# Clearing the pads on VectorE, and weight sums whose plain copies go through SyncE's queue

## The chip, the cores and the metric

The kernel runs on one core of a Trainium2 chip. The metric is the device time of one launch in microseconds. Before the change three runs took 1014.99, 1016.2 and 1018.35 us, so the median is 1016.2 us.

## What is computed

One layer of a streaming encoder over 512 frames and 16 learned meta positions, with a width of 1024. In the reference, cut to what matters here:

```
u = rmsnorm(h);  proj = u @ w_in                  # conv branch, q, k, v, z, decay, beta, gates
c = c_val * sigmoid(c_gate);  c = dwconv31(c);  y_conf = silu(layernorm(c)) @ w_conf_out
q, k, v = split(silu(dwconv4([q, k, v])));  q, k = l2norm(q), l2norm(k)       # 8 heads of 128
o = chunk_gated_delta_rule(q, k, v, g, beta)      # needs inverses of triangular matrices
y_dn = (rmsnorm(o) * silu(z)) @ w_dn_out
h = h + (sigmoid(gA) * y_conf + sigmoid(gB) * y_dn) @ w_out
u2 = rmsnorm(h);  f_gate, f_val = split(dwconv3(u2 @ w_up))
h = h + (silu(f_gate) * f_val) @ w_down;  out = rmsnorm(h)[16:]
```

Everything is fp32.

## The kernel before

**Products.** A weight tile of 128 by 1024 numbers (512 KB) is fetched by SyncE into one of three buffers `wr`. ScalarE rounds it into `wh`, VectorE subtracts to get the rest `wl` (two buffers of each), and TensorE forms a product from three parts: `wh` with the rounded activation, `wh` with its rest, and `wl` with the rounded activation. One weight is 48 matmuls over half of the positions each. In the trace `cv`, `cg`, `q`, `k`, `v`, `z`, `ga`, `y`, `up`, `dn` are accumulators of such products, `wP`, `kS`, `S`, `vp` and `o` belong to the delta rule.

**Sums of weights.** Most tile pairs of the FFN's up projection are formed from seven products in place of eight, and that needs sums of quarters of the weights. `presums` makes 19 such groups of sums in DRAM (tile `ws`) by DMAs alone: two plain copies of 512 KB from the input, then one accumulating copy of 512 KB and two of 256 KB, each behind the one before it. All are started by GpSimd. The sums are read back as weights only in the FFN.

**Pads.** The causal convolution over four positions (`conv4` for q, k and v; `out_raw` for the first seven) reads a row of 528 positions with four zeros ahead of it. The row is the tile `ra`; `G.memset(a[:, :PAD], 0.0)` clears the four on GpSimd, 23 times. VectorE's three multiply-adds `cv<-ra,par,cv` read the row.

**Inverses.** `inverses` solves the triangular matrices by blocks of 32 on VectorE; `grow(h0)` puts the blocks of four heads together (`mn<-DU` copies on GpSimd, then TensorE). After it the heads run: the chain through the state `S`, with `r` on VectorE between two matmuls.

**Order.** The code only records its operations. A planner (`Plan.order`) gives each operation a price and a priority and writes one fixed list per engine; `Plan.emit` issues all of them at L469, so every row of the trace carries that line. `BIAS` moves named parts of the work in priority, `LNP`, `IVP`, `UP` and `WP` are the offsets of the layer norm, the inverses, the normalised input and the weights' splitting, and `SWITCH` is what a change of ScalarE's table costs in the planner. `plan.after` holds an operation back in the planner alone: on the chip an instruction waits for its data, its buffer and what stands ahead of it on its engine or queue. The lines are L538 to L556 (`presums`), L733 (`out_raw`), L854 (`conv4`), L990 (`grow`) and L1210 (the call of `presums`, held by the last mask that GpSimd makes).

Of the kernel before, what the change touches and what calls it, by code (L numbers as in the profile page):

```python
# [30 lines left out]
FT = DFF // P  # L31
EPS = 1e-6
PAD = 4
# [116 lines left out]
AHEAD = {'PE': 3000, 'DVE': 3000, 'ACT': 3000, 'POOL': 400, 'SP': 400}  # L150
KEEP = {"p1": 1, "st": 1, "bt": 2}
STAY = 3000
SWITCH = 375

BIAS = {'tp': 3910, 'h0': 970, 'h2': 370, 'h4': 870, 'h6': 1960, 'sw': 30, 'k3': 0, 'iv': 2100, 'd0': 30, 'v4': 30, 'v2': 0, 'd7': -250, 'z1': 0, 't11': -410, 'z5': 600, 't7': 30, 'k0': 1000, 'ln': 250, 's7': -60, 'z0': -350, 'o2': 250, 'o5': -60, 'd5': -3630, 'g3': -30, 'd6': 0, 'd1': 130, 'k2': 1500, 'q7': -100, 'k5': 600, 's4': -2070, 'd4': -270, 'w3': -1630, 't2': -720, 'c5': -230, 't8': -500, 'v3': -1220, 'o4': -30, 'q6': -250, 'g4': -220, 't4': -600, 'o1': 50, 'q4': -660, 't9': -430, 'z2': -250, 'o0': 3630, 'g0': 0, 'q3': 100, 'q5': 0, 'c1': 30, 'c6': -130, 's1': -1370, 't15': 250, 't1': -540, 's3': 0, 'y0': 150, 't12': -500, 'o6': 850, 'o3': -600, 'k4': 30, 'w2': 2300, 't5': 30, 'v0': 0, 'y2': 0, 'g7': 900, 'g1': 1520, 's6': -940, 'z4': -1680, 't0': 600, 'w0': -430, 'tq': 1880, 't13': 0, 'z6': 30, 'y3': -440, 'd3': -250, 'q2': -130, 't6': 30, 'u18': 150, 't3': -60, 'u6': -230, 'u15': 0, 'u8': -250, 'u17': 100, 'c2': -160, 'g2': 880, 'u1': 0, 'u3': 0, 'u11': 30, 'k1': 0, 'v7': -570, 'w4': -1430, 'u4': -100, 'm4': 0, 'q1': -1780, 't14': -150, 'u9': 0, 'u10': -280, 'u13': 600, 'y7': -130, 'u5': -130, 'm1': 70, 'u20': 0, 'm5': 60, 'u16': 130, 'u12': -250, 'q0': -1500, 'c3': -400, 'u19': 0, 'u14': -250, 'u2': -30, 'v6': 30, 'y6': 30, 'm6': -100, 'z3': 0, 'm0': 0, 'y1': -70, 'y4': -30, 's0': 0, 'g6': 750, 'c4': 0, 'c0': 250, 's5': -1250, 't10': 0, 'm2': 0, 'y5': 0, 'm7': 350, 'm3': 40, 'o7': 0, 'v5': 100, 'k6': 0, 'v1': -250, 'u21': -100, 'd2': -1000, 'u7': 600, 'c7': 0, 'z7': 0, 'g5': 0, 'k7': -70}
LNP = -146
IVP = 2165
UP = 519
WP = 214


WARM = 16
# [21 lines left out]
NPRE = 3  # L184
# [46 lines left out]
class Plan:  # L231
# [10 lines left out]
    def at(self, by, late=True):  # L242
        if isinstance(by, str):
            by, late = BIAS.get(by, 0), False
        was = self.late
# [52 lines left out]
    def price(self, eng, fn, a, k, out):  # L298
        n = out.n
        if eng == "PE":  # L300
            lhs, rhs = (k["lhsT"], k["rhs"]) if fn == "matmul" else (a[1], a[2])
            n = rhs.n
            if fn == "transpose":
                return 110, 0
            if lhs.tl.dt == F32R:

                return RATE * n + 4 + (2 if rhs.ap.offset % rhs.tl.row % 4 else 0), 0
            return max(n, lhs.n) / 0.6 + 8, 0
        if fn == "dma_start":
            if eng == "POOL":  # L310

                return 1000, int(np.prod(out.shape)) * 4 / 140.0
            return 475, int(np.prod(out.shape)) * 4 / 290.0 * (1 if self.run(k) >= P else 2)
        aps = sum(isinstance(k.get(x), Vw) for x in ("scalar", "scalar1", "scalar2", "scale", "bias", "mul"))
        src = [v for x, v in k.items() if x.startswith("in") and isinstance(v, Vw)]
        psum = any(v.tl.space == "psum" for v in src + [out])
        if eng == "ACT":
            return 0.833 * n + (51 if any(v.tl.space == "psum" for v in src) else 93) + 93 * aps + 93 * ("accum_out" in k) + (124 if out.shape[0] in (32, 64) else 0), 0
        if eng == "DVE":
            r = {"reciprocal": 6.3, "tensor_copy": 1.04 if psum else 0.52, "tensor_scalar": 1.04 if psum else 0.52}.get(fn, 1.042)  # L320
            return r * n + 65 + 62 * aps + (134 if fn == "transpose" else 0), 0
        return 1.0 * n + 80, 0

    def order(self):
# [32 lines left out]
        def look(e, t):  # L357

            q, nxt, best = ready[e], later[e][0][0] if later[e] else None, None
            for p, i in q:  # L360
# [111 lines left out]
def record(A, out):  # L472
    plan = Plan(SLOTS)
    V, S, G, PE, SY = (Rec(plan, e) for e in ("DVE", "ACT", "POOL", "PE", "SP"))

    def ext(ap):
        t = Tl(plan, "dram", None, list(ap.shape), F32, "ext")
        t.real = ap
        return Vw(t, ap)

    A = {n: ext(ap) for n, ap in A.items()}
    out = ext(out)
# [4 lines left out]
    def bt(dt=F32, n="bt"):  # L487
        return plan.tile("sb", "bt", [P, ROW], dt, n)
# [21 lines left out]
    def pc(name, i=0, w=1):  # L510
        return par[:, COL[name] + i:COL[name] + i + w]


    def weights(src, n=D):
# [4 lines left out]
        lo = plan.tile("sb", "wl", [P, D], F32R, "wl")  # L519
        with plan.at(WP):  # L520
            S.copy(out=hi[:, :n], in_=w[:, :n])
# [16 lines left out]
    def presums(src, n, hold):  # L538


        r = [plan.tile("dram", "con", [P, 4, HD], F32, "ws") for _ in range(n)]
        for m in range(n):
          with plan.at(1):

            h = {hold} | ({softs[-2]} if len(softs) > 1 else set())
            plan.after = set(h)
            G.dma_start(out=r[m][:, 0:2], in_=src[:, m, 0:3:2])
            plan.after = set(h)
            G.dma_start(out=r[m][:, 2:4], in_=src[:, m, 0:2])
            G.dma_start(out=r[m][:, 1:3], in_=src[:, m, 3:4].broadcast_to([P, 2, HD]), accum_op=ALU.add)  # L550
            G.dma_start(out=r[m][:, 0], in_=r[m][:, 1], accum_op=ALU.add)
            G.dma_start(out=r[m][:, 3], in_=r[m][:, 0], accum_op=ALU.add)
            softs.append(len(plan.ops) - 1)
        return r
# [68 lines left out]
    def split(src, width, n="x"):  # L623
        hi, lo = bt(F32R, n + "h"), bt(F32R, n + "l")
        S.copy(out=hi[:, :width], in_=src)
        V.tensor_tensor(out=lo[:, :width], in0=src, in1=hi.bitcast(F32)[:, :width], op=ALU.subtract)
        return hi, lo
# [24 lines left out]
    def rstd_rows(ss, width, scale, bias, whole=False):  # L652

        q = width // 4
        acc, r = sums(ss, width, whole)
        S.activation(out=r[:, :q], in_=acc[:, :q], func=AF.Sqrt, bias=bias, scale=scale)
        V.reciprocal(out=r[:, :q], in_=r[:, :q])
        return r
# [4 lines left out]
    def halves(ap, w):  # L663
        return ap.rearrange("p (b w) -> p b w", b=2)
# [65 lines left out]

    def out_raw(acc):
        a = bt(n="ra")
        G.memset(a[:, :PAD], 0.0)  # L733
        V.tensor_tensor(out=halves(a[:, PAD:], 264), in0=acc[:, :, :264], in1=halves(rx[:, :T], 264), op=ALU.mult)
        return a

# [2 lines left out]
    for k in range(KT + 1):  # L739
      with plan.at(UP):  # L740
        if k < KT:
# [58 lines left out]
    g2 = g_.rearrange("p n h -> p (n h)")  # L800
# [46 lines left out]
    def conv4(acc, t, way=None):  # L847

        c = bt(n="cv")
        if way:  # L850
            a = acc
            if way == "copy":
                a = bt(n="ra")
                G.memset(a[:, :PAD], 0.0)  # L854
                S.copy(out=halves(a[:, PAD:], 264), in_=acc[:, :, :264])
            cv, src = c[:, :T], lambda j: a[:, 1 + j:1 + j + T]
        else:
            cv, src = halves(c[:, :T], 264), lambda j: acc[:, :, 1 + j:265 + j]
        S.mul(out=cv, in_=src(3), mul=pc('dw', t * 4 + 3))
        for j in (2, 1, 0):  # L860
            V.scalar_tensor_tensor(out=cv, in0=src(j), scalar=pc('dw', t * 4 + j), in1=cv, op0=ALU.mult, op1=ALU.add)
        S.activation(out=c[:, :T], in_=c[:, :T], func=AF.Silu)
        return c
# [76 lines left out]
        for b in range(4):  # L940
            SY.dma_start(out=d_m[b, h].rearrange("n j t -> j n t"), in_=mn[32 * b:32 * b + 32, :, 32 * b:32 * b + 32])

    masks, softs = [], []
    ivt = {}

    def inverses():
# [247 lines left out]
    def call(fn, name, i):  # L1194
        with plan.at(f"{name}{i}"):
            return fn(i)
# [9 lines left out]
    for h in (H - 2, H - 1):  # L1206
        call(decays, "d", h)
        call(grams, "m", h)

    wus = presums(A['wuq'], FT - NPRE, masks[-1])  # L1210
    with plan.at(IVP), plan.at("iv"):
        inverses()
    for f in range(max(sum(GLUS, [])) + 2, KT):
# [10 lines left out]
    for h in range(H):  # L1224
        heads(h)
        if h == 0:
            call(grow, "w", NG)
        for i in OUTS[h]:
            outs(i)
        for i in GATES[h]:  # L1230
            gts[i] = call(gate, "t", i)
# [29 lines left out]

    with plan.at(LNP), plan.at("ln"):
        layer_norm()
# [119 lines left out]
    for f in range(KT - 1):  # L1383
# [3 lines left out]
        o = back(f)  # L1387
# [9 lines left out]
    o, s = back(f), bt(n="fsq")  # L1397
    for b in range(2):
# [9 lines left out]
        r = rstd_rows([sq[:, c], s[:, c]], hw, 1.0 / D, eps)  # L1408
# [97 lines left out]
```

## Time and profile before

| | us |
|---|---|
| median of three runs | 1016.2 |
| the profiled execution | 1018.73 |
| its span | 1016.9 |
| TensorE busy in it | 995.6 |
| VectorE busy | 766.4 |
| ScalarE busy | 526.2 |
| GpSimd busy | 108.4 |

The mean granted clock of TensorE in that execution was 0.994 of full speed. TensorE is busy for 98% of the span, but a busy matmul may be one at a lower clock, or one whose recorded end is modelled; GpSimd's share counts its DMA starts, while the time in which it stands before a DMA for its data to land counts as idle. A part of a microsecond is to be had only where TensorE stands or is slow, so the rows further down are mostly those of such places.

### The profile page before, as it was taken

To read this page: it belongs to the slowest core of one execution; us is meant where nothing else is said; L and a number is where in the kernel's file an instruction comes from. 1 tells how busy PE (TensorE), PEld (TensorE's weight loads), DVE (VectorE), ACT (ScalarE), POOL (GpSimd) and SP (SyncE) were. 2 spreads that over 40 slices of the span, in tenths; PEclk is the share of its full clock that TensorE was granted. 3 is DMA by queue.
4 is the path that set the end of the run, shared out by engine and by line. 5 is a ranking of instruction groups with operands and counts; after the bars stand their busy time and mean duration, and the time that the engine had idled before them with its cause. 6 is when DMAs were issued, how large, how long until landed. Compare 5 with 4: busy or idle time off the path is not lost.

```text
span 1016.9 us, 20105 instructions
## 1 busy us (share of the span) xinstructions
PE 995.6 (98%) x8202; PEld 949.7 (93%) x8202; DVE 766.4 (75%) x1304; ACT 526.2 (52%) x945; POOL 108.4 (11%) x172
## 2 busy tenths in 40 slices
PE   9999999999999999999999999999999999999996
PEld 6999999999989998989999999999999999988886
DVE  5988959689979998989485455599998988832334
ACT  5688732263644554355373224467786766632222
POOL 0011221523421222120000000000000000000000
PEclk9999999999999999999999999999999999999998
DMA  6144698988688897883313244424555556643332
GB/s 224 63 124 97 174 208 218 254 161 191 178 152 203 217 221 158 206 195 87 123 63 110 98 167 138 133 84 145 176 179 184 189 164 185 206 136 101 99 93 83
DMA packets 67932, 157.39 MB, mean 155 GB/s; under 512 B 15104, under 2 KB 21632, under 8 KB 67840
## 3 DMA queue, kind: packets, MB, share of 16 engines
q1 hardware_dynamic: 51728, 116.26, 36.1%
q0 software_dynamic: 16112, 39.85, 20.4%
q8 instruction: 64, 1.05, 0.4%
q14 instruction: 28, 0.23, 0.1%
HBM read 150.78 MB, written 45.16 MB: 193 GB/s over the span
## 4 chain that ended last, share of the span: by engine, by line
PE 72%; DMA 12%; issue 6%; DVE 5%; ACT 3%; POOL 1%; SPq 0%; DVEq 0%; ACTq 0%; POOLq 0%
PE dn L469 12%; PE sx L469 10%; PE y L469 9%; DMA ws<-in_wuq 7%; PE sz L469 7%; PE wo L469 5%; PE cv L469 5%; PE ga L469 4%; PE cg L469 4%; PE up L469 3%; PE z L469 2%; PE v L469 2%; DMA ws<-ws 2%; DMA eg<-d_e 2%; PE q L469 2%
## 5 line engine op out<-in xcount | busy, mean ns | idle before, releaser
L469 DVE TENSOR_TENSOR wl<-wr,wh 128x1024 fp32r<-128x1024 f32 (+2 forms) x195 | 225.6, 1158 | 156.0 <-PE dn L469 61.6
L469 ACT CAST wh<-wr 128x1024 fp32r<-128x1024 f32 (+2 forms) x195 | 193.8, 996 | 222.0 <-PE dn L469 56.4
L469 DVE SCALAR_TENSOR_TENSOR ca<-c,par,ca 128x516 f32<-128x516 f32 (+10 forms) x240 | 178.4, 750 | 6.3 <-ACT ca L469 2.3
L469 DVE SCALAR_TENSOR_TENSOR uy<-up,par,uy 128x512 f32<-128x512 f32 x88 | 64.2, 746 | 1.8 <-ACT uy L469 1.4
L469 POOL DMA_DIRECT2D ws<-in_wuq x57 | 49.3, 872 | 151.3 <-DMA ws<-in_wuq 77.7
L469 PE MATMUL dn<-fh,wh 128*128 128x512 f32 (+1 forms) x171 | 61.8, 369 | 0.0
L469 PE MATMUL dn<-fl,wh 128*128 128x512 f32 (+1 forms) x171 | 61.8, 369 | 0.0
L469 PE MATMUL sx<-nh,wh 128*128 128x258 f32 x228 | 60.5, 289 | 1.2 <-ACT wh L469 0.9
L469 PE MATMUL sz<-nl,wh 128*128 128x258 f32 x228 | 59.8, 283 | 0.0
L469 PE MATMUL sx<-nl,wh 128*128 128x258 f32 x228 | 59.4, 282 | 0.0
L469 PE MATMUL sz<-nh,wh 128*128 128x258 f32 x228 | 59.4, 283 | 0.0
L469 PE MATMUL ga<-ul,wh 128*128 128x258 f32 (+1 forms) x256 | 59.0, 294 | 0.0
L469 PE MATMUL ga<-uh,wh 128*128 128x258 f32 (+1 forms) x256 | 58.7, 294 | 0.0
L469 DVE SCALAR_TENSOR_TENSOR cv<-ra,par,cv 128x528 f32<-128x528 f32 x69 | 50.8, 758 | 6.2 <-POOL ra L469 5.9
L469 PE MATMUL ga<-uh,wl 128*128 128x258 f32 (+1 forms) x256 | 48.4, 295 | 0.0
L469 POOL DMA_DIRECT2D ws<-ws x38 | 35.8, 951 | 93.6 <-DMA ws<-in_wuq 58.8
L469 PEld LDWEIGHTS sx<-nh,wh 128*128 128x128 f32 x228 | 43.1, 189 | 2.9 <-ACT wh L469 1.4
L469 PE MATMUL sz<-nh,wl 128*128 128x258 f32 x228 | 44.6, 283 | 0.0
L469 PEld LDWEIGHTS sx<-nl,wh 128*128 128x128 f32 x228 | 43.2, 190 | 0.0
L469 PEld LDWEIGHTS sz<-nh,wh 128*128 128x128 f32 x228 | 42.9, 189 | 0.1
L469 PEld LDWEIGHTS sz<-nl,wh 128*128 128x128 f32 x228 | 42.9, 189 | 0.0
L469 PEld LDWEIGHTS ga<-ul,wh 128*128 128x128 f32 x256 | 42.7, 192 | 0.3
(324 smaller groups left out, 2764.7 us busy)
## 6 DMA issues: line engine op xcount, KB each, us to landing
wr<-in_win SPq DMA_DIRECT2D x64, 512.0 KB
ws<-in_wuq POOLq DMA_DIRECT2D x57, 512.0 KB, 7.9
wr<-ws SPq DMA_DIRECT2D x38, 512.0 KB
ws<-ws POOLq DMA_DIRECT2D x38, 256.0 KB, 6.1
wr<-in_wuq SPq DMA_DIRECT2D x19, 512.0 KB
wr<-in_wd SPq DMA_DIRECT2D x17, 512.0 KB
wr<-in_wuq SPq DMA_DIRECT2D x19, 256.0 KB
wr<-in_wdn SPq DMA_DIRECT2D x8, 512.0 KB
```

The source lines that it names most:

```text
L469: getattr(engines[o.eng], o.fn)(*(get(x) for x in o.a), **{n: get(x) for n, x in o.k.items()})
```

## The change

The pads are cleared by VectorE. The two plain copies of each group of sums are started by SyncE, in the queue that also carries the weights; the three accumulating ones stay on GpSimd. `presums` is called in the loop over the heads, after the second `grow`, and is held in the planner by the last operation that GpSimd has been given by then, its last copy of the inverses' blocks. The planner's price of a DMA started by GpSimd, `SWITCH`, the offsets and all of `BIAS` are other numbers, so that the order changes on every engine.

```diff
-SWITCH = 375
-BIAS = {'tp': 3910, 'h0': 970, 'h2': 370, 'h4': 870, 'h6': 1960, 'sw': 30, 'k3': 0, 'iv': 2100,
...
-LNP = -146
-IVP = 2165
-UP = 519
-WP = 214
+SWITCH = 600
+BIAS = {'tp': 800, 'h0': 300, 'h2': 300, 'h4': 300, 'h6': 300, 'sw': -60, 'k3': -2020, 'iv': -1500,
...
+LNP = 0
+IVP = 1165
+UP = 0
+WP = 44
...
             if eng == "POOL":
-                return 1000, int(np.prod(out.shape)) * 4 / 140.0
+                return 1000, int(np.prod(out.shape)) * 4 / 122.0
...
             plan.after = set(h)
-            G.dma_start(out=r[m][:, 0:2], in_=src[:, m, 0:3:2])
+            SY.dma_start(out=r[m][:, 0:2], in_=src[:, m, 0:3:2])
             plan.after = set(h)
-            G.dma_start(out=r[m][:, 2:4], in_=src[:, m, 0:2])
+            SY.dma_start(out=r[m][:, 2:4], in_=src[:, m, 0:2])
             G.dma_start(out=r[m][:, 1:3], in_=src[:, m, 3:4].broadcast_to([P, 2, HD]), accum_op=ALU.add)
...
     def out_raw(acc):
         a = bt(n="ra")
-        G.memset(a[:, :PAD], 0.0)
+        V.memset(a[:, :PAD], 0.0)
...
             if way == "copy":
                 a = bt(n="ra")
-                G.memset(a[:, :PAD], 0.0)
+                V.memset(a[:, :PAD], 0.0)
...
-    masks, softs = [], []
+    masks = []
...
-    wus = presums(A['wuq'], FT - NPRE, masks[-1])
     with plan.at(IVP), plan.at("iv"):
         inverses()
...
         if h == 0:
             call(grow, "w", NG)
+            softs = []
+            wus = presums(A['wuq'], FT - NPRE, max(i for i, o in enumerate(plan.ops) if o.eng == "POOL"))
```

GpSimd, in the middle of the sums, before the change. `ws` are the sums, `in_wuq` the FFN's weights, `ra` a row whose pad is cleared.

```order
L469 DMA ws_3520<-in_wuq 128x2x512
L469 DMA ws_3546<-in_wuq 128x2x512
L469 DMA ws_3520<-ws_3520 128x512
L469 DMA ws_3546<-ws_3546 128x512
L469 DMA ws_3520<-ws_3520 128x512
L469 MEMSET ra_2071 128x4
L469 DMA ws_3546<-ws_3546 128x512
L469 DMA ws_3988<-in_wuq 128x2x512
```

The pad stands behind accumulating copies that each wait for the copy before. VectorE, after the change, at a row of the same kind (`wl` is the rest of a weight, `r` the delta rule's step):

```order
L469 TENSOR_TENSOR wl_5594<-wr_5205,wh_5486 128x1024
L469 SCALAR_TENSOR_TENSOR r_27_5611<-kS_5601,egn_809,v_5399 128x128
L469 SCALAR_TENSOR_TENSOR r_28_5618<-kS_5599,egn_809,v_5319 128x128
L469 MEMSET ra_5597 128x4
L469 SCALAR_TENSOR_TENSOR cv_5605<-ra_5597,par_82,cv_5605 128x528 x3
L469 TENSOR_TENSOR o_6_5653<-o_6_5653,q_7_4979 128x516
L469 TENSOR_TENSOR o_7_5659<-o_7_5659,q_8_4985 128x516
```

The pad is now cleared on the engine that reads it, among the work of the same row.

SyncE's queue before the change, behind the 33rd of the weights (`eg` is a row of decays that comes back from DRAM):

```order
L469 DMA wr_3010<-in_win 128x1024
L469 DMA wr_3098<-in_win 128x1024
L469 DMA eg_3130<-d_e_872 128x528
L469 DMA wr_3261<-in_win 128x1024
L469 DMA wr_3302<-in_win 128x1024
L469 DMA wr_3434<-in_win 128x1024
L469 DMA eg_3608<-d_e_872 128x528
L469 DMA wr_3611<-in_win 128x1024
```

And after it, from the 36th weight on, where the first sums start:

```order
L469 DMA wr_3088<-in_win 128x1024
L469 DMA ws_3128<-in_wuq 128x2x512
L469 DMA ws_3158<-in_wuq 128x2x512
L469 DMA ws_3128<-in_wuq 128x1024
L469 DMA ws_3158<-in_wuq 128x1024
L469 DMA wr_3458<-in_win 128x1024
L469 DMA wr_3487<-in_win 128x1024
L469 DMA eg_3600<-d_e_919 128x528
L469 DMA eg_3602<-d_e_919 128x528
L469 DMA ws_3643<-in_wuq 128x2x512
L469 DMA ws_3686<-in_wuq 128x2x512
L469 DMA ws_3643<-in_wuq 128x1024
```

Four plain copies of 512 KB stand between the 36th weight and the 37th; the 38 of them are spread up to the 76th.

TensorE where the sums of the layer norm begin (`rs<-ca`; `ca` are the 31-tap convolution's outputs), before the change:

```order
L469 MATMUL ga_6320<-uh_113,wl_6328 128x260
L469 MATMUL ga_6320<-uh_117,wl_6328 128x258
L469 MATMUL ga_6320<-uh_117,wl_6328 128x260
L469 MATMUL ga_6320<-uh_125,wl_6328 128x258
L469 MATMUL ga_6320<-uh_125,wl_6328 128x260
L469 MATMUL rs_6388<-ca_5753,ones_65 32x129 x4
L469 MATMUL rs_6388<-ca_5246,ones_65 32x129 x4
```

And after it:

```order
L469 MATMUL z_5765<-uh_99,wl_5692 128x258
L469 MATMUL rs_5897<-o_4_4764,hsel_71 32x129 x4
L469 MATMUL rs_5897<-o_6_5653,hsel_71 32x129 x4
L469 MATMUL rs_5897<-o_7_5659,hsel_71 32x129 x4
L469 MATMUL rs_5897<-o_8_5878,hsel_71 32x129 x4
L469 MATMUL rs_5915<-ca_4905,ones_65 32x129 x4
L469 MATMUL rs_5915<-ca_4391,ones_65 32x129 x4
```

The layer norm's sums now follow right behind those of the delta rule's outputs `o`. Counted over the whole list, they stand behind 63.4 groups of 48 weight matmuls before the change and behind 56.3 after it, and 62 subtractions `wl` of VectorE stood ahead of the last tap of `ca`, where 54 do now.

## Rows read from the trace of the kernel before

**Rows 1.** The page: busy us, share, instructions.

```profile
PE 995.6 (98%) x8202; PEld 949.7 (93%) x8202; DVE 766.4 (75%) x1304; ACT 526.2 (52%) x945; POOL 108.4 (11%) x172
```

**Rows 2.** Windows: stretch, length, busy per engine (count), PEclk, DMA share, GB/s.

```profile
100.00:484.80 384.80, 376.83 (x3441) 365.65 (x3441) 336.13 (x608) 184.49 (x384) 100.83 (x149) 0.99 0.80 188
```

**Rows 3.** Timeline, 293 to 298: start, us, operation, [idle before <- releaser].

```profile
293.30 0.81 POOL L469 DMA_DIRECT2D ws<-ws  x1 [5.14 <-DMA ws<-in_wuq]
...
294.00 0.28 PE L469 MATMUL ga<-uh,wl 128*128 128x260 f32 x1
...
295.10 0.39 POOL L469 MEMSET ra<- 128x4 f32 x1
...
295.53 0.77 DVE L469 SCALAR_TENSOR_TENSOR cv<-ra,par,cv 128x528 f32<-128x528 f32 x1 [2.83 <-POOL ra L469]
...
296.61 0.49 PE L469 MATMUL wP<-r,mn 128*128 128x128 f32 x2 [2.33 <-DVE r L469]
```

**Rows 4.** Windows of 3 us behind the two stalls.

```profile
296.00:299.00 3.00, 2.39 (x16) 2.37 (x17) 3.00 (x7) 1.74 (x5) 0.14 (x1) 0.85 0.99 85
299.00:302.00 3.00, 3.00 (x18) 3.00 (x18) 2.05 (x4) 1.22 (x2) 1.42 (x2) 0.58 0.80 68
395.00:398.00 3.00, 0.67 (x3) 0.67 (x4) 2.96 (x5) 0.64 (x1) 0.00 (x0) 0.84 1.08 167
398.00:401.00 3.00, 3.00 (x17) 2.82 (x15) 2.86 (x5) 2.13 (x6) 1.30 (x2) 0.59 1.07 261
```

**Rows 5.** Timeline, 394 to 398: the second stall.

```profile
397.33 0.90 PE L469 MATMUL vp<-cst,cv 128*128 128x128 f32 x3 [2.37 <-ACT cv L469]
```

**Rows 6.** Tile `ra`, GpSimd's part: ns min/median/max, first and last start.

```profile
L469 POOL MEMSET ra<- x23: 101/120/909, 1.2 to 426.6; 128x4 f32 x23
```

**Rows 7.** Waits of DVE in the whole span.

```profile
DVE cv L469 <- POOL ra L469: 5.9, 3, 2.8
...
DVE cv L469 <- DMA eg<-d_e: 3.5, 2, 2.4
```

**Rows 8.** Timeline: the shortest memset of VectorE.

```profile
1.05 0.09 DVE L469 MEMSET ss<- 128x40 f32 x1
```

**Rows 9.** Timeline: first and last start for the sums, first reading.

```profile
113.80 0.87 POOL L469 DMA_DIRECT2D ws<-in_wuq  x1
...
461.31 0.81 POOL L469 DMA_DIRECT2D ws<-ws  x1 [4.10 <-DMA ws<-ws]
...
677.50 0.33 SPq L469 DMA_DIRECT2D wr<-ws  x1
```

**Rows 10.** Waits of SyncE's queue: what it stood before longest.

```profile
SPq L469 <- DVE wl L469: 656.8, 157, 18.0
```

**Rows 11.** Timeline: the first weight; the 36th to 38th; chain: one weight.

```profile
2.12 0.43 SPq L469 DMA_DIRECT2D wr<-in_win  x1
...
7.17 1.04 ACT L469 CAST wh<-wr 128x1024 fp32r<-128x1024 f32 x1 [1.63 <-DMA wr<-in_win]
...
243.84 11.63 SPq L469 DMA_DIRECT2D wr<-in_win  x3
...
163.00 5.87 PE cv L469 x48
```

**Rows 12.** The page's DMA queues (packets, MB, share) and issues (KB, us to landing).

```profile
q1 hardware_dynamic: 51728, 116.26, 36.1%
q0 software_dynamic: 16112, 39.85, 20.4%
...
ws<-in_wuq POOLq DMA_DIRECT2D x57, 512.0 KB, 7.9
```

**Rows 13.** Timeline: last taps of `ca`, first sums `rs<-ca`; page: the `wl` group.

```profile
481.72 3.06 DVE L469 SCALAR_TENSOR_TENSOR ca<-c,par,ca 128x501 f32<-128x501 f32 x4
500.13 1.09 PE L469 MATMUL rs<-ca,ones 128*32 128x129 f32 x32
...
L469 DVE TENSOR_TENSOR wl<-wr,wh 128x1024 fp32r<-128x1024 f32 (+2 forms) x195 | 225.6, 1158 | 156.0 <-PE dn L469 61.6
```

More of the change, by code (lines that the diff above doesn't have):

```diff
@@ L152 @@
 STAY = 3000
-SWITCH = 375
-BIAS = {'tp': 3910, 'h0': 970, 'h2': 370, 'h4': 870, 'h6': 1960, 'sw': 30, 'k3': 0, 'iv': 2100, 'd0': 30, 'v4': 30, 'v2': 0, 'd7': -250, 'z1': 0, 't11': -410, 'z5': 600, 't7': 30, 'k0': 1000, 'ln': 250, 's7': -60, 'z0': -350, 'o2': 250, 'o5': -60, 'd5': -3630, 'g3': -30, 'd6': 0, 'd1': 130, 'k2': 1500, 'q7': -100, 'k5': 600, 's4': -2070, 'd4': -270, 'w3': -1630, 't2': -720, 'c5': -230, 't8': -500, 'v3': -1220, 'o4': -30, 'q6': -250, 'g4': -220, 't4': -600, 'o1': 50, 'q4': -660, 't9': -430, 'z2': -250, 'o0': 3630, 'g0': 0, 'q3': 100, 'q5': 0, 'c1': 30, 'c6': -130, 's1': -1370, 't15': 250, 't1': -540, 's3': 0, 'y0': 150, 't12': -500, 'o6': 850, 'o3': -600, 'k4': 30, 'w2': 2300, 't5': 30, 'v0': 0, 'y2': 0, 'g7': 900, 'g1': 1520, 's6': -940, 'z4': -1680, 't0': 600, 'w0': -430, 'tq': 1880, 't13': 0, 'z6': 30, 'y3': -440, 'd3': -250, 'q2': -130, 't6': 30, 'u18': 150, 't3': -60, 'u6': -230, 'u15': 0, 'u8': -250, 'u17': 100, 'c2': -160, 'g2': 880, 'u1': 0, 'u3': 0, 'u11': 30, 'k1': 0, 'v7': -570, 'w4': -1430, 'u4': -100, 'm4': 0, 'q1': -1780, 't14': -150, 'u9': 0, 'u10': -280, 'u13': 600, 'y7': -130, 'u5': -130, 'm1': 70, 'u20': 0, 'm5': 60, 'u16': 130, 'u12': -250, 'q0': -1500, 'c3': -400, 'u19': 0, 'u14': -250, 'u2': -30, 'v6': 30, 'y6': 30, 'm6': -100, 'z3': 0, 'm0': 0, 'y1': -70, 'y4': -30, 's0': 0, 'g6': 750, 'c4': 0, 'c0': 250, 's5': -1250, 't10': 0, 'm2': 0, 'y5': 0, 'm7': 350, 'm3': 40, 'o7': 0, 'v5': 100, 'k6': 0, 'v1': -250, 'u21': -100, 'd2': -1000, 'u7': 600, 'c7': 0, 'z7': 0, 'g5': 0, 'k7': -70}
@@ L156 @@
-LNP = -146
-IVP = 2165
-UP = 519
-WP = 214
+SWITCH = 600
+BIAS = {'tp': 800, 'h0': 300, 'h2': 300, 'h4': 300, 'h6': 300, 'sw': -60, 'k3': -2020, 'iv': -1500, 'd0': -100, 'v4': -30, 'v2': 0, 'd7': 300, 'z1': 0, 't11': 0, 'z5': 600, 't7': 0, 'k0': -250, 'ln': 250, 's7': 0, 'z0': -700, 'o2': -250, 'o5': -1430, 'd5': -1250, 'g3': 50, 'd6': -250, 'd1': 1750, 'k2': -30, 'q7': -1790, 'k5': -60, 's4': -980, 'd4': 850, 'w3': -1600, 't2': -630, 'c5': 0, 't8': -290, 'v3': 500, 'o4': -600, 'q6': -250, 'g4': -350, 't4': -100, 'o1': 500, 'q4': -630, 't9': 0, 'z2': -600, 'o0': -600, 'g0': 30, 'q3': 250, 'q5': 0, 'c1': 280, 'c6': -130, 's1': 0, 't15': 30, 't1': 30, 's3': 100, 'y0': 250, 't12': -150, 'o6': 1500, 'o3': -600, 'k4': -100, 'w2': 150, 't5': 0, 'v0': 280, 'm3': 0, 'o7': 100, 't6': 280, 'm4': -30, 's6': -30, 'g7': -380, 'u9': 0, 'z4': 500, 'z6': 100, 'w0': -250, 'y3': 100, 't3': -250, 'u14': 30, 'v7': 250, 'u18': 0, 'z3': 0, 'd2': -30, 'u6': 0, 'tq': 100, 'd3': 30, 'm5': -70, 'm2': 0, 'y7': 0, 'g5': 30, 'y4': -30, 'v6': 0, 'u19': 0, 'v5': 250, 's5': 0, 'y5': -250, 'u13': -30, 'u20': 0, 'k6': -30}
```

## The prediction

> **What bounds the kernel now.** I read the page's shares first, then TensorE's waits and the windows around them, then VectorE's waits, then the queues. TensorE is busy for 995.6 of 1016.9 us [rows 1], so all that can be won without less work of its own is 21.3 us of idle time and the places where its clock is low. The change leaves its products alone. What is to be seen in the windows from 100 to 484.8 us, the stretch in which the heads and the sums of weights run, is an engine hardly behind it: VectorE is busy for 336.1 of 384.8 us, 87%, and idle for 48.7 us [rows 2]. GpSimd is busy for 100.8 us there, and most of the rest it stands before a DMA.
>
> Two stalls of TensorE in that stretch are longer than 2 us. The first ends at 296.61, when `wP` starts after 2.33 us without work because `r` on VectorE came late [rows 3]. `r` came late because VectorE, in order, had stood for 2.83 us before `cv<-ra`, and that ended with GpSimd's clearing of the pad at 295.10 [rows 3]. GpSimd had itself stood for 5.14 us before a DMA of the sums, and the pad is behind those in its list. Behind the stall the granted clock is 0.85 in the first 3 us and 0.58 in the next [rows 4]: a mixture of the two levels, 2.4 and 1.2 GHz, after TensorE had stood. Against full speed that is 3 x 0.15 + 3 x 0.42 = 1.7 us. So this stall costs 2.33 + 1.7 = 4.0 us.
>
> The second ends at 397.33, 2.37 us long, before `vp<-cst,cv` [rows 5]. In that window VectorE is busy for 2.96 of 3 us and GpSimd for none [rows 4], so it is VectorE's own lag. The clock behind it is 0.84 and 0.59: 3 x 0.16 + 3 x 0.41 = 1.7 us, together 4.1 us.
>
> **Part 1: the pads.** GpSimd loses 23 memsets of a median 0.12 us [rows 6], VectorE gains 23. What goes is the wait for GpSimd, 5.9 us of VectorE's time in three places [rows 7], and of it the one that reached TensorE: -4.0 us. What is late next there: after VectorE's `r`, nothing in the row shows another engine behind, so I take all of it. No row shows a memset of four columns on VectorE; one of 40 columns takes 0.09 us [rows 8]. The bounds are 0 (VectorE is idle for 48.7 us in the stretch and the memset has no input to wait for) and 23 x 0.09 = 2.1 us (all of them on the path). VectorE is near enough to the bound that I take a third of it, +0.8 us.
>
> **Part 2: the plain copies on SyncE's queue.** 38 starts of 0.33 to 0.43 us [rows 9, 11] are 13 to 16 us of a queue that stands 656.8 us in all before it may overwrite a weight [rows 10]; they cost nothing by themselves. The risk is behind them. A weight's DMA now stands behind up to four copies of 512 KB. The first weight needs 7.17 - 2.12 = 5.05 us from issue to ScalarE's cast [rows 11], and with three buffers it is started about three weights of 5.87 us ahead [rows 11], so the cover is 17.6 - 5.05 = 12.6 us. How long four copies hold it up is bounded by two rows. The queue of the hardware kind moved 116.26 MB in 36.1% of the span, 367 us: 317 GB/s while busy, so 0.524 MB is 1.65 us and four are 6.6 us, under the cover. The median landing of such a copy on the old queue is 7.9 us [rows 12]; four one behind the other would be 31.6 us, 19.0 us past the cover. I take the first, as the copies go one behind another without a wait between them: 0 us, with 6.0 us of slack. The upper end stays as a rival.
>
> The old queue, software_dynamic, moved 39.85 MB in 20.4% of the span, 207 us, or 192 GB/s [rows 12], and its mix has the accumulating copies in it. The Trainium skill ("DMA: Bandwidth & Descriptors", section "Issuing engines are not separate DMA queues") says that DMAs started by ScalarE, SyncE or GpSimd end up on the same 16 engines and interleave, so that another starter saves only the start. By it the copies would be as slow as on the old queue: 2.7 us each, 10.9 us for four, and 1.7 us of slack instead of 6.0. By the rule as by the rows the sum gets 0, but by the rule one more DMA among them would be late.
>
> GpSimd loses 38 of its 95 DMA starts. Its accumulating copies now wait for copies of another queue, and what stands behind them in its list is only more of them, since both `grow`s now come ahead. Nobody waits for it then until the sums are read.
>
> **Part 3: the sums start later.** They begin at 113.80 and the last starts at 461.31 [rows 9], 347.5 us. Now the first stands behind the 36th weight, which was issued at 243.84 [rows 11]. The same length from there ends at 591; the first reading is at 677.50 [rows 9]. 86 us of room, so 0 us. It would cost if the chain became a quarter longer.
>
> **Part 4: the order.** The place to look at is the layer norm. Its sums stand 63.4 - 56.3 = 7.1 weights earlier, 7.1 x 5.87 = 41.7 us: 500.13 would become 458.4 [rows 13]. All taps of `ca` must be done by then. VectorE's list before that point gets 62 - 54 = 8 subtractions of 1.16 us shorter [rows 13], 9.3 us, and 1.6 us of pads longer (18 or so of the 23, taken with their 0.09): 336.1 - 9.3 + 1.6 = 328.4 us of work in 358.4 us. VectorE may then idle for 30.0 us where it idled for 48.7. I take it that it does, because 5.9 us of waits for pads and much of the lag go, and price it at 0; the rival below is the other end. The second stall was VectorE's lag; with another order I give half of it back, -2.0 us, bounded by 0 and -4.1. The `eg` rows are consumed in two places soon after their issue, as they were before, when VectorE stood 3.5 us for two of them [rows 7]; I take 0, between -3.5 and +3. ScalarE is busy for 184.5 of 384.8 us [rows 2], which hides any reordering of it.
>
> **Sum.** -4.0 - 2.0 + 0.8 + 0 + 0 + 0 = -5.2 us. The profiled execution took 1018.73 us, 2.5 above the median, so the forecast from it is 1013.5 for such an execution, and 1016.2 - 5.2 = 1011 us for the median of runs.
>
> **Rivals.** *Nothing to be had, 1016 us.* The stalls of before are two incidents in a long list; another order makes its own. For it: VectorE is as full as it was, and one stall of 2.4 us with its clock behind it eats 4.1 us. Against it: the pad's stall has a cause that the change takes away. With one such stall of its own and a microsecond of smaller ones, -5.2 + 4.1 + 1.1 = 0: 1016 us.
>
> *VectorE becomes the bound, 1024 us.* If VectorE idles ahead of the layer norm as it did before, it lacks 48.7 - 30.0 = 18.7 us, and TensorE, in order, stands for that, there or at the delta rule's steps on the way. For it: 87% busy, and much of its idle time is forced by waits for TensorE and ScalarE within a head. It decides from the point where VectorE idles for more than 30.0 us before the last tap. With 70% of the lack, 13 us: 1011 + 13 = 1024; with all of it, 1030.
>
> *The weights come late, 1030 us.* The copies take the cover of 12.6 us, as they do at a landing of 7.9 us each: 1011 + 19.0 = 1030 for the group of four; the three groups of three would add 3 x (23.7 - 12.6) = 33 us if they did the same. Against it: the rate of the queue while busy.
>
> *The change doesn't do what it says*, if the sums' plain copies held up the accumulating ones so long that the FFN waits: by part 3 it has 86 us of room, and I give it no chance of its own.
>
> **How the numbers follow.** The forecast has 0.47, nothing to be had 0.27, VectorE 0.20, late weights 0.06. What a measurement of this kernel can tell from no change is 0.3%, 3.05 us, so faster means under 1013.2 and slower over 1019.2. The forecast's own bounds are 1011 - 2.1 - 3.5 - 0.8 = 1004.6 and, with nothing of the second stall, all of the pads and the `eg` rows, 1011 + 2.0 + 1.3 + 3 = 1017; most of it is below 1013.2, and what is above is balanced by the better half of the second case. So faster 0.47, same 0.27, slower 0.26. The range goes from 1004 to 1026: it takes in the forecast, the second case and the nearer half of the third, and leaves out some 0.16. The likeliest case alone is 1005 to 1017.
>
> **What the profile of the changed kernel would show.** Part 1: no wait of `cv` on VectorE for GpSimd, and no stall of `wP` with such a cause. Part 2: ScalarE's cast not waiting for a weight's DMA between 240 and 560 us; if it waits for several us there, the third rival is right. Part 3: the first plain copy near 245 us, the last accumulating one near 590 and in any case before 677. Part 4: `rs<-ca` near 458 us; if it starts later than 465 with TensorE idle before it, or `wP` and `vp` wait often for VectorE, the second rival is right. The granted clock should have fewer 3-us stretches under 0.9 between 200 and 450 us. The prediction is wrong in its reasons if the time is won at another place than 294 and 397 us, above all in the FFN, where I expect no difference.

## The result: 1003.5 us, more than twice the gain that was forecast

Four runs of the changed kernel took 1001.06 to 1004.99 us, 1003.53 in the median, beside 1015.6 for four of before: a ratio of 0.9875 with a 95% interval of 0.9846 to 0.9905. That is 12.1 us where 5.2 were forecast, and the time lies below the range. A second set, on another chip, gave 1001.0 against 1016.1 (0.9864, 0.9832 to 0.9896). The profiled execution took 1001.06 us, the fastest of its four, and that of before 1018.73, above all four of its runs, so the two spans (999.3 and 1016.9) lie further apart than the medians. Three executions in the later sets, one each of before (1596.61 us), a_neither (5426.38) and b_start (1184.56), lie far above all others and are left out of the medians and ratios below.

The page of the kernel after, its busy times, which answer to [rows 1]:

```profile
PE 986.7 (99%) x8202; PEld 945.3 (95%) x8202; DVE 760.0 (76%) x1327; ACT 522.1 (52%) x941; POOL 79.1 (8%) x111
```

TensorE does the same 8202 instructions in 8.9 us less busy time, and its idle time is 12.6 us instead of 21.3. Its waits over the whole span, after (us in all, times, longest):

```profile
PE warm L469 <- DVE eps L469: 1.1, 1, 1.1
PE rb L469 <- DVE rr L469: 1.0, 1, 1.0
PE sx L469 <- ACT up L469: 1.0, 1, 1.0
PE rs L469 <- ACT fsq L469: 1.0, 1, 1.0
PE o L469 <- DVE cv L469: 0.9, 1, 0.9
PE sz L469 <- DVE nl L469: 0.6, 1, 0.6
PE gg L469 <- ACT junk L469: 0.3, 1, 0.3
PE vp L469 <- ACT cv L469: 0.2, 1, 0.2
```

Of the stalls of [rows 3] and [rows 5] nothing is left: no wait for `r`, and 0.2 us before `vp`. None of 2 us has come in their place. The windows of VectorE's stretch (columns as in [rows 2]), first after and then before:

```profile
100.00:200.00 100.00, 99.97 (x817) 98.95 (x816) 99.81 (x248) 39.85 (x84) 2.17 (x4) 1.00 0.32 101
100.00:443.00 343.00, 341.80 (x3192) 332.31 (x3194) 317.65 (x611) 170.84 (x362) 54.65 (x74) 1.00 0.68 163
```

```profile
100.00:200.00 100.00, 100.00 (x820) 99.25 (x819) 76.28 (x217) 44.23 (x95) 26.87 (x43) 1.00 0.85 210
```

VectorE is now busy for 99.8 of the 100 us from 100 on, where it was busy for 76.3; it works ahead, and the DMA engines are at 0.32 there, since the sums have not begun. The last tap of `ca` and the first `rs<-ca`, and the first `rc` (the first product with the inverse norms) of the kernel after, from the timeline:

```profile
415.63 1.50 DVE L469 SCALAR_TENSOR_TENSOR ca<-c,par,ca 128x499 f32<-128x499 f32 x2
...
443.11 1.94 PE L469 MATMUL rs<-ca,ones 128*32 128x129 f32 x64
```

```profile
22.93 1.06 PE L469 MATMUL rc<-rr,cst 128*128 128x132 f32 x8
```

The layer norm's sums begin 57 us earlier than in [rows 13], and VectorE has been done with the taps for 26 us. The sums of weights after, by tile (count, ns min/median/max, first and last start):

```profile
L469 SPq DMA_DIRECT2D ws<-in_wuq x38: 522/614/1962, 227.6 to 536.7; - x38
L469 POOL DMA_DIRECT2D ws<-ws x38: 814/824/1363, 246.4 to 560.6; - x38
L469 SPq DMA_DIRECT2D wr<-ws x38: 326/326/329, 654.6 to 852.2; - x38
```

The first starts at 228 us and the last at 561, 94 us ahead of the first reading. The pad on VectorE, two views of the kernel after, tile and timeline:

```profile
L469 DVE MEMSET ra<- x23: 62/62/62, 25.3 to 419.5; 128x4 f32 x23
```

```profile
25.31 0.42 DVE L469 TENSOR_TENSOR abT<-ab,rx 128x264 f32<-128x264 f32 x1
25.33 0.06 DVE L469 MEMSET ra<- 128x4 f32 x1
```

Its 62 ns lie wholly beside the end of the work ahead of it.

The prediction named the FFN as the place where it expected no difference. The windows from the first product of the up projection (`up`) to the end, of before, after and b_pads_start (below; before, in its order, with two edits), columns as in [rows 2]:

```profile
649.09:1016.90 367.81, 357.54 (x2544) 333.37 (x2542) 261.80 (x392) 203.53 (x313) 0.00 (x0) 0.99 0.46 144
```

```profile
633.66:999.30 365.64, 355.81 (x2544) 332.86 (x2542) 262.68 (x392) 203.44 (x313) 0.00 (x0) 0.99 0.47 145
```

```profile
634.45:1002.30 367.85, 357.54 (x2544) 333.70 (x2542) 261.88 (x392) 203.48 (x313) 0.00 (x0) 0.99 0.44 144
```

So 2.2 us of the 17.6 between the two spans are won in the FFN, by the same 2544 matmuls. In the traces of the kernels below, that of b_start left out, the same stretch takes 365.0 to 367.5 us in the new order and 365.9 to 369.7 in the old; what makes the difference is not shown.

### The profile page after: what moved, and what is told of

Same layout as the page of the kernel before. It is cut to its first block, busy times and chain, and to the rows that moved or that the text cites. A ratio compares the mean times of both kernels' runs of the same rounds, so it can differ in the third digit from the quotient of the medians.

```text
span 999.3 us, 20081 instructions
## 1 busy us (share of the span) xinstructions
PE 986.7 (99%) x8202; PEld 945.3 (95%) x8202; DVE 760.0 (76%) x1327; ACT 522.1 (52%) x941; POOL 79.1 (8%) x111
## 3 DMA queue, kind: packets, MB, share of 16 engines
q8 instruction: 64, 1.05, 0.4%
## 4 chain that ended last, share of the span: by engine, by line
PE 89%; DVE 7%; ACT 2%; DMA 1%; issue 1%; DVEq 0%; ACTq 0%
PE dn L469 12%; PE y L469 9%; PE sx L469 9%; PE ga L469 9%; PE sz L469 7%; PE k L469 5%; PE z L469 5%; PE wo L469 5%; PE cv L469 5%; PE q L469 4%; PE cg L469 4%; PE v L469 4%; PE o L469 2%; DVE wl L469 1%; PE rs L469 1%; PE up L469 1%
## 5 line engine op out<-in xcount | busy, mean ns | idle before, releaser
L469 DVE TENSOR_TENSOR wl<-wr,wh 128x1024 fp32r<-128x1024 f32 (+1 forms) x195 | 225.9, 1158 | 157.5 <-PE dn L469 60.6
L469 ACT CAST wh<-wr 128x1024 fp32r<-128x1024 f32 (+1 forms) x195 | 194.1, 996 | 228.9 <-PE dn L469 59.8
L469 DVE SCALAR_TENSOR_TENSOR ca<-c,par,ca 128x516 f32<-128x516 f32 (+12 forms) x240 | 176.9, 745 | 2.0
L469 PE MATMUL sx<-nh,wh 128*128 128x258 f32 x228 | 57.9, 285 | 1.2 <-ACT up L469 1.0
L469 PE MATMUL sz<-nl,wh 128*128 128x258 f32 x228 | 57.4, 283 | 0.6 <-DVE nl L469 0.6
L469 PE MATMUL ga<-uh,wl 128*128 128x258 f32 (+1 forms) x256 | 43.8, 288 | 0.0
L469 PEld LDWEIGHTS ga<-uh,wh 128*128 128x128 f32 x256 | 42.0, 189 | 1.0 <-issue 0.6
L469 PE MATMUL dn<-fh,wl 128*128 128x512 f32 (+1 forms) x171 | 39.8, 369 | 0.0
```

Of the source, the lines that this page charges most:

```text
L469: getattr(engines[o.eng], o.fn)(*(get(x) for x in o.a), **{n: get(x) for n, x in o.k.items()})
```

## Experiments

The first question was which part won: the new order of all engines (theory A), the engines that the change names (B), or the later sums (D). The first kernels below keep a planner's order and give single instructions to another engine when they are issued, so that no list moves but for that; where a list is changed too, it is said. The edits are written short. The condition `pad` stands for `o.fn == "memset" and o.tiles[0].name == "ra"`, and `plain` for a DMA into `ws` without an `accum_op`. Ratios are to the kernel before in the same set, with 95% intervals.

**b_pads.** Before, with the pads on VectorE alone.

```diff
+                e = "DVE" if pad else o.eng
-                getattr(engines[o.eng], o.fn)(...)
+                getattr(engines[e], o.fn)(...)
```

> The kernel before, every list in its old order, only the 23 pads are cleared by VectorE where GpSimd cleared them. Theory A (the new order of all engines wins most of the time): only the stall of wP at 294 us and its slow clock go, about 4 us, so 1011 to 1013; the stalls before vp at 395 and 437 us stay. Theory B (VectorE's 5.9 us of waits for GpSimd are what put VectorE behind everywhere): the stalls at 395 and 437 shrink too, 1005 to 1008. If the pad's stall only moves elsewhere: 1015 to 1017.

1009.7 us, ratio 0.9944 (0.9916 to 0.9971). The stalls of TensorE in the heads are gone with the order unchanged; its waits for VectorE and ScalarE between 100 and 500 us in b_pads are these two:

```profile
PE o L472 <- DVE cv L472: 1.3, 1, 1.3
...
PE vp L472 <- ACT cv L472: 0.3, 1, 0.3
```

By the time this is nearer to A, 1.3 us below its forecast; by the trace it is B, since the stalls at 395 and 437 us, which the prediction put down to VectorE's own lag, went too. That is weak support for B: before_again, below, lacks these two with the pads still on GpSimd.

**b_both.** Before, in its order, with the pads on VectorE and the plain copies on SyncE's queue.

```diff
+                e = "DVE" if pad else "SP" if plain else o.eng
```

> The kernel before in its old order, with the 23 pads on VectorE and the 38 plain copies of the sums started by SyncE at their old places in the program, so from about 114 us on. Theory A (order): no better than the pads alone, 1011 to 1013. Theory B (the engines that the change names): nearly all of the gain, 1003 to 1006. Theory C (weights late behind plain copies): casts wait for weights, 1016 or more.

1011.2 us, ratio 0.9955 (0.9930 to 0.9981): as the pads alone, so the plain copies bring nothing, and B falls as a whole. Weights were not late either; ScalarE's longest wait for one was 1.3 us. Its trace (1015.23 us, one of the two longest of its ten) has the stall before `vp` again, though no pad is on GpSimd. VectorE and then TensorE in b_both:

```profile
383.86 0.76 DVE L474 SCALAR_TENSOR_TENSOR orb<-o,par,orb 128x516 f32<-128x516 f32 x1 [3.84 <-DMA orb<-d_r]
```

```profile
398.11 1.11 PE L474 MATMUL vp<-cst,cv 128*128 128x128 f32 x4 [3.19 <-ACT cv L474]
```

**a_neither.** The changed kernel's order with both undone.

```diff
+                e = "POOL" if pad or plain else o.eng
```

> The changed kernel in its new order, but the pads cleared by GpSimd again and all copies of the sums started by GpSimd again. Theory A (order): most of the gain stays, 1004 to 1008, with a few waits of cv for GpSimd. Theory B (engines): the gain goes, 1013 or more.

1015.58 us, ratio 1.0002 (0.9982 to 1.0022). Theory A falls: the new order by itself is worth nothing. With the pads on GpSimd it has stalls of its own, VectorE and then TensorE at the longer of two in a_neither:

```profile
286.72 1.45 DVE L474 SCALAR_TENSOR_TENSOR cv<-ra,par,cv 128x528 f32<-128x528 f32 x2 [5.07 <-POOL ra L474]
```

```profile
288.90 1.01 PE L474 MATMUL qk<-cv,cv 128*128 128x128 f32 x3 [4.88 <-ACT cv L474]
```

**b_pads_late.** b_pads, with GpSimd's list changed: its DMAs for the sums stand behind its last copy of the inverses.

```diff
+            idx = [i for i in idx[:n + 1] if i not in ws] + ws + [i for i in idx[n + 1:] if i not in ws]
```

> The kernel before in its old order with the pads on VectorE, and in GpSimd's list all 95 DMAs of the sums moved behind its last copy of the inverses' blocks (about 261 us), all of them still started by GpSimd. Theory A (order): as the pads alone within 2 us. Theory D (with the sums out of the way early, weights, decays and GpSimd's copies come sooner): 3 us or more under the pads alone; the waits for eg at 237 us go first. If the sums end too late: the last accumulating copy beyond 640 us and a wait before the first reading of ws.

1014.6 us, ratio 0.9984 (0.9961 to 1.0007). The sums ran from 202 to 541 us. The expectation took its place from before, where the last copies stood at 261 us. Theory D falls: in this order later sums lose most of what the pads gave. Of the 4.1 us by which its trace ends behind that of b_pads, 2.1 are lost near 485 us, where VectorE stood 4.2 us for a late row `orb`, and the rest from 710 us on; why is not shown.

That left two new theories. E: the pads behind GpSimd's DMAs are what the heads lose, in either order. F: the start is won by fewer changes between narrow and full matmuls. The next four kernels test them.

**a_padsback.** The changed kernel with the pads back on GpSimd.

```diff
+                e = "POOL" if pad else o.eng
```

> The changed kernel in its new order, plain copies of the sums still on SyncE's queue, but the pads cleared by GpSimd again. Theory E (the pads behind GpSimd's DMAs are what the heads lose, in either order): waits of cv for GpSimd come back and TensorE stands 5 us or more for cv or r, 1010 to 1014. If it was the plain copies on GpSimd that hurt the new order: 1004 to 1006.

1015.5 us, ratio 1.001 (0.9995 to 1.0024), 1.5 us beyond the slow end of what E gave. With the pads back on GpSimd the whole gain is gone. One pad shows how, VectorE and then TensorE in a_padsback:

```profile
318.65 0.77 DVE L472 SCALAR_TENSOR_TENSOR cv<-ra,par,cv 128x528 f32<-128x528 f32 x1 [5.85 <-POOL ra L472]
```

```profile
323.31 2.07 PE L472 MATMUL qk<-cv,cv 128*128 128x128 f32 x8 [5.60 <-ACT cv L472]
```

**a_plainback.** The changed kernel with the plain copies back on GpSimd.

```diff
+                e = "POOL" if plain else o.eng
```

> The changed kernel in its new order with the pads on VectorE, but all copies of the sums started by GpSimd. Theory E: which queue carries the plain copies is worth nothing, 1002 to 1006. If SyncE's queue is part of the gain: 1008 or more, with the sums ending later than 560 us or waits for weights and decays.

1004.3 us, ratio 0.9892 (0.9844 to 0.9940), as the changed kernel. Which queue starts the plain copies is worth nothing that can be measured, though the sums end 14 us later (last start 574.8).

**b_pads_start.** b_pads, with TensorE's list ahead of the first `rc` rewritten: the narrow matmuls wait until 10 stand together. The new list, `pe`, is written out by number (shortened here).

```diff
-            for i in self.order():
+            idx, pe = self.order(), [3, 4, 5, ...]
...
+            lists["PE"] = pe + lists["PE"]
```

> The kernel before in its old order with the pads on VectorE, and of TensorE's list ahead of the first rc the narrow matmuls (ab and rs, 32 columns of output) are held back until 10 of them stand together: 10 changes between narrow and full matmuls where there were 20. Theory F (the changed kernel wins 3 us in its first 25 us because it changes less often between the two): rc starts 1 to 2 us earlier than 25.6, and the time is 1 to 2 us under the 1009.7 of the pads alone. If the changes cost nothing: rc at 25.6 and 1009 to 1011.

1004.3 us, ratio 0.9895 (0.9858 to 0.9933). The first `rc` of b_pads and of b_pads_start:

```profile
25.68 1.06 PE L472 MATMUL rc<-rr,cst 128*128 128x132 f32 x8
```

```profile
22.05 1.06 PE L480 MATMUL rc<-rr,cst 128*128 128x132 f32 x8
```

3.6 us, twice what F expected, and every later matmul that was compared between the two traces starts 3.6 to 5.0 us earlier. The direction is F's; the size was set too low, because fewer changes are only a part of what the groups win (last section). The old order with two edits comes within the noise of the changed kernel.

**a_start.** The same on the changed kernel, in groups of 12 or more: 8 changes for 14.

```diff
+            idx, pe = self.order(), [3, 4, 5, ...]
...
+            lists["PE"] = pe + lists["PE"]
```

> The changed kernel with the narrow matmuls ahead of the first rc held back until 12 of them stand together: 8 changes between narrow and full matmuls where it has 14. Theory F: rc about 1 us earlier than 22.9 and 1002 to 1003; if changes cost nothing, 1003 to 1004.

1002.5 us, ratio 0.9876 (0.9834 to 0.9917), `rc` at 22.30: 0.6 us earlier instead of 1, because `k` then waits 0.7 us, mostly for `wh`, and the warm-up matmuls ended 0.6 us later in this trace.

**b_start.** The batched start with the pads still on GpSimd, that is b_pads_start without its first edit.

```diff
-                e = "DVE" if pad else o.eng
```

> The kernel before with the pads still on GpSimd, and only the narrow matmuls ahead of the first rc held back until 10 stand together (10 changes for 20). Theory F (the changes between narrow and full matmuls at the start are paid on their own, and what is won there is carried to the end): rc 3.6 us earlier than 25.6, 1011 to 1012, and the stall of wP for the pad stays. If later waits for DMAs swallow it: 1013 to 1016.

1012.19 us, ratio 0.9970 (0.9944 to 0.9995). The same kernel, for its trace, is **b_start_again**:

> The kernel before with the narrow matmuls of the start in groups of 10, pads on GpSimd, for a trace: rc near 22 us, 3.6 us earlier than before, and the stall of wP for the pad near 290 as before.

`rc` came at 22.10, and the pad took most of the start's gain back: TensorE is 2.9 us ahead of before at 292 us and 0.6 at 301. GpSimd and then TensorE at the pad in b_start_again, with VectorE's wait between them:

```profile
293.55 0.80 POOL L477 DMA_DIRECT2D ws<-ws  x1 [1.65 <-DMA ws<-ws]
294.07 0.39 POOL L477 MEMSET ra<- 128x4 f32 x1
```

```profile
294.49 0.77 DVE L477 SCALAR_TENSOR_TENSOR cv<-ra,par,cv 128x528 f32<-128x528 f32 x1 [4.72 <-POOL ra L477]
...
295.58 0.80 PE L477 MATMUL wP<-r,mn 128*128 128x128 f32 x2 [4.21 <-DVE r L477]
```

The pad is cleared 1.0 us earlier than in before, where TensorE came 2.9 us earlier; so it stands the longer before the same pad, 4.21 us for 2.33. Whether the two gains add up is not settled. By the medians the start is worth 4.0 us with the pads on GpSimd and 5.4 with them on VectorE, which the intervals don't tell apart; and in this trace TensorE is 5.6 us ahead again by 445 us, because the two later stalls, which are behind rows and not pads, were shorter.

**b_noacc.** Before, pads on GpSimd, without the accumulating copies.

```diff
+                if "accum_op" in o.k:
+                    continue
```

> The kernel before with the pads still on GpSimd and without the accumulating copies, so that the sums of weights are left unsummed and GpSimd waits for no copy of its own. Theory E (a pad is late only because GpSimd stands in order before the copies it has to add to): the waits of cv for GpSimd all but go, with the pads where they were, 1006 to 1010. If it is GpSimd's own starts that delay the pads: waits of 2 us or more stay, 1012 to 1016.

1008.2 us, ratio 0.9926 (0.9899 to 0.9952), as E says. VectorE waits for no pad any more. What GpSimd's sums still wait for, in b_noacc:

```profile
POOL ws L472 <- issue: 11.8, 12, 4.4
```

So it isn't GpSimd that is slow at a pad, nor its starts, but its standing, in order, before the copies it adds to. The run also takes away DMA traffic, which isn't separated here.

**before_again** and **b_pads_again** asked whether the stalls at 395 and 437 were chance.

> The kernel before once more, for a second trace. If the stalls follow from the list alone: 2.3 us before wP near 294, 2.4 before vp near 395 and 2.0 before vp near 437 again. If the last two are landings that vary: the one at 294 again within 0.5 us, the other two gone or of another size, and a span 2 to 6 us shorter.

> The kernel before with the pads on VectorE, for a second trace: no wait of wP near 291; stalls before vp only where a row's DMA lands late, under 2 us each. If the pads make the rows land earlier, none over 0.5 us, as in the first trace.

1016.6 and 1006.8 us. In before_again `wP` stood 1.7 us, those two were gone, and another had come, VectorE and then TensorE:

```profile
375.14 2.81 DVE L469 SCALAR_TENSOR_TENSOR cv<-ra,par,cv 128x528 f32<-128x528 f32 x4 [2.58 <-POOL ra L469]
```

```profile
379.96 1.40 PE L469 MATMUL qk<-cv,cv 128*128 128x128 f32 x6 [2.21 <-ACT cv L469]
```

In all, VectorE waited 8.4 us for pads in four places there, and 5.9 in three in [rows 7]. In b_pads_again nothing over 0.3 us stood before `vp`, and no `wP`. So both expectations of the second traces half hold: which pad stalls, and for how long, varies; that some do, doesn't.

**after_again** and **a_start_again**, on the same chip:

> The changed kernel once more, beside the next one: 1002 to 1005.

> The changed kernel with the narrow matmuls ahead of the first rc in groups of 12 (8 changes for 14), against the changed kernel on the same chip: 0.6 to 1 us under it, since rc came 0.6 us earlier.

1001.0 and 1000.1 us; ratios 0.9864 (0.9832 to 0.9896) and 0.9850 (0.9824 to 0.9877). The order of the two is as expected both times, but their intervals overlap, so that the batched start beats the changed kernel is not shown.

One mark stands in all kernels of the old order, the first `rs<-ca`; its start in each trace sums up the heads and the start, late rows included:

| kernel | pads | start | first `rs<-ca`, us |
|---|---|---|---|
| before | GpSimd | old | 500.13 |
| before_again | GpSimd | old | 497.75 |
| b_start_again | GpSimd | batched | 494.47 |
| b_pads | VectorE | old | 490.42 |
| b_pads_again | VectorE | old | 488.52 |
| b_pads_start | VectorE | batched | 485.44 |

## Why the prediction was wrong, step by step

**Two steps failed. The first is in part 1**, "of it the one that reached TensorE: -4.0 us". That stall was read rightly: in the trace of b_pads TensorE gains 4.2 us on before at that `wP` (comparing the starts of the same matmuls), where 4.0 were added up. But one stall of one trace was taken for all that the 23 pads cost, and it was taken from the old order, while the forecast is for the new one. Off GpSimd they are worth 5.5 us by the medians of b_pads (2.9 to 8.5 by its interval) and 11 to 12 us in the new order (a_padsback against a_plainback and against the changed kernel). The forecast for this part was -4.0 + 0.8. By places, counting the stall and the slow clock behind it: in the first pair of traces (before and b_pads) 4.7 us go at two pads, in the second (before_again and b_pads_again) 6.7 at three, and in a_padsback against the changed kernel 9.1 at two. The mark lies 9.7 and 9.2 us apart in the two pairs; what is above the pads' part came at late rows and other places, and is not shown to be the pads'.

**The second is in part 4 and in the zeros of the sum**: an order that is new on every engine was priced in the heads alone. The start was put at nothing, and b_pads_start shows what was there: 5.4 us under b_pads by the medians of their sets, 4.7 by the spans of the traces, 3.6 of it before the first `rc`.

**What made VectorE's lag look like the cause** was one row that the prediction left out. "It is VectorE's own lag" was concluded from a full VectorE and an idle GpSimd in the 3 us at the stall. Twelve microseconds earlier VectorE had stood, in the timeline of before:

```profile
383.10 0.76 DVE L469 SCALAR_TENSOR_TENSOR orb<-o,par,orb 128x516 f32<-128x516 f32 x1 [3.16 <-DMA orb<-d_r]
```

The DMA of that row was started at 371.57 and VectorE went on 11.5 us later. In b_pads the same instruction follows its predecessor without a wait, at 376.01, 8.4 us after the DMA's start. The stall at 437 stands behind a wait of 2.39 us for `eg` in the same way. In before_again neither row made a stall, and the pad at 375 made one instead. So from 290 us on VectorE has little slack: its waits of 2.83, 3.16 and 2.39 us came through to TensorE as 2.33, 2.37 and 1.96. It is not so all along: at 210 us a wait of 2.40 us for a pad came through as 0.41. The -2.0 us, half of that stall, was a price for a late row, which no order was shown to bring or to take away. That the rows landed earlier without the pads on GpSimd looks like chance: in b_both, with the pads on VectorE, the same row was used 12.6 us after its DMA's start, later than in before.

**Part 1's cost was too high.** 23 memsets were priced at +0.8 us within 0 and 2.1, as a third of the latter, which is 0.7. They take 62 ns each, nearly all of them beside other work: the lower bound.

**Part 2 was right.** ScalarE waited 3.1 us in all for weights and sums, where it waited 3.8 for weights of `w_in` before, a_plainback shows that the queue is worth nothing, and b_both the same in the old order. The rival of late weights did not come true, in either order. The page's DMA queues of a_plainback and of the changed kernel, which differ only in who starts the plain copies (columns as in [rows 12]):

```profile
q1 hardware_dynamic: 51728, 116.26, 35.8%
q0 software_dynamic: 16112, 39.85, 21.1%
```

```profile
q1 hardware_dynamic: 59632, 136.19, 43.6%
q0 software_dynamic: 10640, 19.93, 14.4%
```

The 38 copies take 67.6 us of the old queue's time (211.5 - 143.9) and add 76.8 to SyncE's (435.7 - 358.9): 1.8 and 2.0 us each. So the prediction's 1.65 us was a little low, and the 2.7 of the old queue was that of its mix. The rule weighed there, from the Trainium skill ("DMA: Bandwidth & Descriptors", section "Issuing engines are not separate DMA queues"), that all starters share 16 engines, agrees with this: another starter did not make the copies faster.

**Part 3 was right.** The sums begin at 228 (forecast 245), their last DMA starts at 561 (591), ahead of a first reading at 654.6.

**Part 4 was right about the layer norm and wrong about the start.** `rs<-ca` begins at 443 instead of 458, and VectorE does not lack the 18.7 us of the second rival: it idles for 25.4 us between 100 and 443, under the 30.0 that it was given. The first 25 us are worth 2.6 us in the changed kernel, where `rc` starts at 22.93. TensorE's timeline of before:

```profile
8.64 1.08 PE L469 MATMUL ab<-x,wab 128*32 128x264 f32 x4 [0.87 <-DMA x<-in_xT]
...
25.55 0.73 PE L469 MATMUL rc<-rr,cst 128*128 128x132 f32 x5
```

0.87 us of it is a wait for `x` that has gone. The rest goes with the narrow matmuls (`ab`, `rs`) standing in larger groups between the full ones (`k`): 14 changes between the two for 20, and more narrow ones side by side (last section). The prediction did not draw on the Trainium skill here, which says ("TensorEngine Tiling (Array Packing)", section "Key Properties") that a change of the tiling mode drains TensorE. The traces agree in that the steps at a change are longer, by about 0.15 us a change, below.

**The signs that the prediction named** came out so: no wait for a pad, no cast waiting for a weight between 240 and 560 us, and a granted clock of 1.00 from 100 to 443 us in the row above, all as said. But its last test fails, that the time is not won at another place than 294 and 397 us, above all not in the FFN: 2.6 us are won at the start and 2.2 in the FFN. So its reasons cover a part of the gain.

**The rivals.** *Nothing to be had* is what the new order gives by itself (a_neither, 1015.58), for the reason that the rival gives, stalls of its own; it was the pads off GpSimd that turned it.

**The account.** In the old order the pads alone are worth 5.5 us and the pads with the grouped start 10.6 (b_pads_start, 0.9895), where the changed kernel has 12.1 (0.9875 and 0.9864). The intervals do not tell the last two apart. The traces do so far as one each can: the changed kernel's span is 3.0 us shorter than that of b_pads_start, 2.3 of it in the FFN, where the other traces differ by as much. So what the new order adds beside the start and the pads is small, and its cause stays open.

## What to carry to other kernels

A tiny instruction that is put on an idle engine is late if that engine waits, in order, for its own DMAs; the price isn't its 0.1 us but can be the wait ahead of it, and it moves from run to run. Before a stall is put down to a full engine, follow that engine's own idle time back some 15 us, not 3. And where an order changes everywhere, see in it too how narrow matmuls stand, in the start above all, where they are many: in large groups they cost less than one by one among full ones.

## What the runs showed of the hardware

**Narrow matmuls in groups.** From the first matmul after the warm-up to the first `rc`, waits left out, the same 145 matmuls took 18.2 us in b_pads (25.68 - 6.65 - 0.83) and 13.8 in b_pads_start (22.05 - 8.21), 4.4 us less. At `rc` 3.6 of them show, since the warm-up ended 1.2 us later there and 0.4 us of waits went. The beginnings of the two stretches:

```profile
6.65 0.85 PE L472 MATMUL ab<-x,wab 128*32 128x264 f32 x3
...
8.79 1.08 PE L472 MATMUL ab<-x,wab 128*32 128x264 f32 x4 [0.83 <-DMA x<-in_xT]
```

```profile
8.21 0.51 PE L480 MATMUL k<-xh,wh 128*128 128x264 f32 x2 [0.39 <-ACT wh L480]
```

Two things make up the 4.4 us. The first is the changes between 128 and 32 output columns, in b_pads:

```profile
13.50 0.41 PE L472 MATMUL k<-xh,wh 128*128 128x264 f32 x2
13.75 0.29 PE L472 MATMUL k<-xl,wh 128*128 128x264 f32 x1
13.96 0.66 PE L472 MATMUL rs<-sq,ones 128*32 128x132 f32 x16
14.55 0.39 PE L472 MATMUL k<-xl,wh 128*128 128x264 f32 x1
14.78 0.41 PE L472 MATMUL k<-xh,wh 128*128 128x264 f32 x2
15.03 0.28 PE L472 MATMUL k<-xl,wh 128*128 128x264 f32 x1
```

Among full ones a step from start to start is 0.12 us (two in the 0.25 from 13.50 to 13.75). The step into the narrow ones is 0.21, the one back about 0.1 over the usual, and the first step after it 0.23: some 0.3 us there and back, 0.15 a change. Ten changes fewer are then about 1.4 us of the 4.4, an estimate from these steps.

The other 3 us are won among the narrow ones themselves, which run side by side when more of them stand together. Four `ab` in b_pads and eight in b_pads_start, which start in pairs 0.01 to 0.03 us apart, take the same time:

```profile
20.01 1.08 PE L472 MATMUL ab<-x,wab 128*32 128x264 f32 x4
```

```profile
17.84 1.08 PE L480 MATMUL ab<-x,wab 128*32 128x264 f32 x8
```

All 32 `ab` keep TensorE busy for 8.62 us in b_pads, 7.02 in the changed kernel and 5.03 in b_pads_start. No run changes the number of changes and leaves the groups' size, so the split is by the steps in the traces alone.

None of this shows as a wait: in the first 25 us of before TensorE's only idle times are 1.05 us at the start and the 0.87 above.
